# Decay masks of a chunked state-space scan: one-sum broadcasts by DMA and a ScalarE bias in place of selector matmuls

## The chip, the cores and the metric

The kernel runs on one core of a Trainium2 chip. The metric is the device time of one execution in microseconds. The engines named below are PE (TensorE matmuls), PEld (TensorE weight loads), DVE (VectorE), ACT (ScalarE), POOL (GpSimd) and SP (SyncE, which only issues DMAs here).

## The reference: what is computed

One decoder layer over 1024 positions and 1024 channels: a layer norm, a wide input projection, two parallel mixers (a gated 31-tap convolution and a Mamba-2 scan), a gated sum with an output projection and a layer norm, and then a convolutional feed-forward block. The change touches the scan alone:

```
a = dt * a_head                               # (chunk, position, head), all negative
a_cs = cumsum(a over the 128 positions of a chunk)
seg[l, s] = a_cs[l] - a_cs[s]
decay = where(l >= s, exp(seg), 0)            # per head
y_diag = (C B^T * decay) @ (x * dt)           # per group of 8 heads
y_off  = exp(a_cs) * (C @ state)
state  = exp(a_cs[last]) * state + (B * exp(a_cs[last] - a_cs))^T (x * dt)
```

There are 32 heads in 4 groups of 8, a head has 64 channels, a state has 128 rows, and a chunk has 128 positions, so 8 chunks.

## The kernel before, in words

The sequence is worked in two halves of 512 positions (4 chunks each), index `hh`. For each half, `mixers` (L653) makes the projections of the input. A projection of 128 channels is 24 matmuls of 128x512: 8 blocks of the inner dimension, each as three products of a high and a low part in the format float32r (`mm3`, L193 to 198; `project`, L200). Weights are loaded by SP, copied to the high part by ACT (L172) and subtracted to the low part by DVE (L173), into tiles that rotate over three buffers.

After the first columns, `time_steps` (L308) makes the time steps and, with `upper`, the running sums `a_cs` of every head (L361). It forms `a` with every head repeated four times, so that the 128 rows of the sum are (group, kind 0 to 3, head). The sum is split into a high part (L373) and a low part (L375), and two tables come out of it: `seg_mv` (negated high and low parts, and ones) and `seg_st` (ones, and high and low parts), by L378 and L381.

For each of the four groups the mixer then makes its columns, the gates of the other mixer's convolution (`glu`), and `ssd_group` (L507), which loops over the half's four chunks. Per chunk and group (32 of them in all) it does this:

- PE transposes x and B (L531, L534) and multiplies B with C (L537) into PSUM.
- POOL makes, for group 0, the moving operand `au` (128x1024): `seg_mv` kept in the rows of each head and zeroed elsewhere (L540); it is stored to DRAM (L546) and loaded again for groups 1 to 3 (L548). ACT makes the stationary operand `sg` (L550), the rows of `seg_st` of this group.
- Two matmuls of 128x512 (L554) select and add: their result is `a_cs[s] - a_cs[l]` for 8 heads. ACT applies Relu out of PSUM (L562) and Exp with scale -1 (L563) to the tile `m`, 128x1024. Relu keeps the exponent at zero above the diagonal, where the mask is zero anyway.
- DVE masks B C^T by `upper` (L565), scales x (L567, L572) and multiplies `m` with the masked product (L575). PE multiplies with the state (L580), makes the new state (L584) and multiplies `m` with x (L594, 8 heads).

At the head of each group, `ys` is loaded with exp(a_cs), broadcast over partitions from the DRAM tile `e_scr` (L513); `normed` later passes a row through DRAM and back (L632, L633). These and the loads of `au` are all issued by POOL, in one order. The convolution of 31 taps (`conv31`, L483, 480 instructions on DVE) runs with a lower priority between all this, and `combine` reads its result.

The order of the instructions on every engine is made by a planner, which simulates the program with a cost model and gives each engine a fixed order by priorities and by when an operand would be ready; weight loads have a high priority. Only the PE order of the feed-forward's first part is written by hand. An engine works its list in order, and a waiting instruction holds back what stands behind it.

Of the kernel before, what the change touches and what calls it, by code (L numbers as in the profile page):

```python
# [8 lines left out]
F32 = mybir.dt.float32  # L9
# [45 lines left out]
def kernel(  # L55
# [30 lines left out]
    def bank(which):  # L86
# [18 lines left out]
    V.memset(ones, 1.0)  # L105
    eps = const.tile([P, 1], F32, name="eps")
    V.memset(eps, EPS)
    head_of = const.tile([P, GROUPS, 8], F32, name="head_of")
    V.tensor_reduce(
        out=head_of,  # L110
        in_=ident.rearrange("p (g k h) -> p g h k", k=4, h=8),
        axis=AX.X,
        op=ALU.add,
    )
    lanes = statep.tile([P, 16], F32, name="lanes")
    head_all, group_of = lanes[:, :8], lanes[:, 8:12]
    V.tensor_reduce(
        out=head_all, in_=head_of.rearrange("p g h -> p h g"), axis=AX.X, op=ALU.add
    )
    V.tensor_reduce(out=group_of, in_=head_of, axis=AX.X, op=ALU.add)  # L120
    kind = const.tile([P, 4], F32, name="kind")
    V.tensor_reduce(
        out=kind, in_=ident.rearrange("p (g k h) -> p k g h", k=4, h=8), axis=AX.XY, op=ALU.add
    )
    kind_mv = const.tile([P, 1], F32, name="kind_mv")
    V.tensor_add(kind_mv, kind[:, 2:3], kind[:, 3:4])
    kind_st = const.tile([P, 1], F32, name="kind_st")
    V.tensor_add(kind_st, kind[:, 0:1], kind[:, 1:2])
    kind_neg = const.tile([P, 2], F32, name="kind_neg")
    V.tensor_scalar_mul(kind_neg, kind[:, 0:2], -1.0)  # L130
    pc = const.tile([P, PC_N + 24], F32, name="pc")
    a_log = statep.tile([P, HEADS], F32, name="a_log")
    nskip = statep.tile([P, 2, 16], F32, name="nskip")
    pick = statep.tile([P, 4, 4], F32, name="pick")
# [1 line left out]
    for c in range(4):  # L136
# [7 lines left out]
    states = [statep.tile([P, HALF], F32, name=f"state{g}") for g in range(GROUPS)]  # L144
    dts = [statep.tile([P, 4, HEADS], F32, name=n) for n in ("dtv", "wds")]
    edc = statep.tile([P, 2, 4, HEADS], F32, name="edc")
    seg_mv = statep.tile([P, 4, P], F32, name="seg_mv")
    seg_st = statep.tile([P, 4, P], F32R, name="seg_st")

    h_scr = [dram.tile([HALF, D], F32, name=f"h_scr{i}") for i in range(2)]  # L150
    h1_scr = dram.tile([T, D], F32, name="h1_scr")
# [5 lines left out]
    )  # L157
    c_scr = [dram.tile([8, P, HALF], F32, name=f"c_scr{i}") for i in range(2)]
    g_scr = [dram.tile([8, P, HALF], F32, name=f"g_scr{i}") for i in range(2)]
    e_scr = [dram.tile([P, HALF], F32, name=f"e_scr{i}") for i in range(2)]  # L160
    au_scr = [
        [dram.tile([P, 8 * P], F32R, name=f"au_scr{i}_{c}") for c in range(4)] for i in range(2)
    ]
    r_scr = [dram.tile([GROUPS, HALF], F32, name=f"r_scr{i}") for i in range(2)]
    y_scr = [dram.tile([8, P, HALF], F32, name=f"y_scr{i}") for i in range(2)]

# [141 lines left out]
    def time_steps(pl, hh, ps):  # L308

        n2 = 2 * HEADS  # L310
        dtc = pl.tile([n2, HALF], F32, tag="yo", bufs=2, name=f"dtc{hh}")
        A.activation(
            out=dtc, in_=ps[:n2, :], func=AF.Identity, bias=pc[:n2, PC_DTB : PC_DTB + 1]
        )
        pt = bank(0)
        for c in range(4):
            TE.matmul(
                pt[:, c * HEADS : (c + 1) * HEADS],
                dtc[:, c * P : (c + 1) * P],
                fold,  # L320
                start=True,
                stop=True,
            )
        n = 4 * HEADS
        dtv, wds = (d.rearrange("p c h -> p (c h)") for d in dts)
        work = pl.tile([P, 8 * P], F32, tag="m", name=f"sp{hh}")
        v, s, s2, q, a = (work[:, i * n : (i + 1) * n] for i in range(5))
        ea = work[:, 5 * n : 6 * n + HEADS]
        e = ea[:, :n]
        V.tensor_scalar_mul(ea[:, n:], a_log, -1.0)  # L330
        V.tensor_copy(v, pt[:, :n])
        A.activation(out=e, in_=v, func=AF.Abs)
        A.activation(out=ea, in_=ea, func=AF.Exp, scale=-1.0)
        V.tensor_scalar_add(s, e, 2.0)
        V.reciprocal(out=s, in_=s)
        V.tensor_mul(s, s, e)
        V.tensor_mul(s2, s, s)
        V.tensor_scalar(
            out=q, in0=s2, scalar1=1.0 / 17.0, scalar2=1.0 / 15.0, op0=ALU.mult, op1=ALU.add
        )  # L340
        for k in (13, 11, 9, 7, 5, 3):
            V.tensor_mul(q, q, s2)
            V.tensor_scalar_add(q, q, 1.0 / k)
        V.tensor_mul(q, q, s2)
        V.scalar_tensor_tensor(out=q, in0=q, scalar=1.0, in1=s, op0=ALU.add, op1=ALU.mult)
        V.tensor_scalar_max(v, v, 0.0)
        V.scalar_tensor_tensor(out=dtv, in0=q, scalar=2.0, in1=v, op0=ALU.mult, op1=ALU.add)
        V.scalar_tensor_tensor(
            out=a.rearrange("p (c h) -> p c h", c=4),
            in0=dts[0],  # L350
            scalar=-1.0,
            in1=ea[:, n:].unsqueeze(1).to_broadcast([P, 4, HEADS]),
            op0=ALU.mult,
            op1=ALU.mult,
        )
        ax = pl.tile([P, 4, GROUPS, 4, 8], F32, tag="xs", name=f"sp_ax{hh}")
        for k in range(4):
            A.copy(ax[:, :, :, k, :], a.rearrange("p (c g h) -> p c g h", c=4, g=GROUPS))
        pa = bank(0)
        for c in range(4):  # L360
            TE.matmul(  # L361
                pa[:, c * P : (c + 1) * P],
                ax[:, c].rearrange("p g k h -> p (g k h)"),
                upper,
                start=True,
                stop=True,
            )
        eh = pl.tile([P, HALF], F32, tag="yo", bufs=2, name=f"sp_eh{hh}")
        A.activation(out=eh, in_=pa, func=AF.Exp)
        G.dma_start(e_scr[hh], eh)  # L370
        hi = pl.tile([P, HALF], F32R, tag="xsd", name=f"sp_hi{hh}")
        lo = pl.tile([P, HALF], F32, tag="sig", name=f"sp_lo{hh}")
        V.tensor_copy(hi, pa)  # L373
        hi = hi.bitcast(F32)
        V.tensor_tensor(out=lo, in0=pa, in1=hi, op=ALU.subtract)  # L375
        for dst, m, const_m in ((seg_mv, kind_neg, kind_mv), (seg_st, kind[:, 2:4], kind_st)):
            part = pl.tile([P, HALF], F32, tag="ya", bufs=2, name=f"sp_part{hh}")
            V.tensor_scalar(  # L378
                out=part, in0=hi, scalar1=m[:, 0:1], scalar2=const_m, op0=ALU.mult, op1=ALU.add
            )  # L380
            V.scalar_tensor_tensor(  # L381
                out=dst.rearrange("p c l -> p (c l)"),
                in0=lo,
                scalar=m[:, 1:2],
                in1=part,
                op0=ALU.mult,
                op1=ALU.add,
            )
        pe = bank(0)
        for i, m in enumerate((later, ones)):  # L390
            TE.matmul(pe[:, i * n : (i + 1) * n], m, a, start=True, stop=True)
        ev = edc.rearrange("p i c h -> p (i c h)")
        A.activation(out=ev, in_=pe[:, : 2 * n], func=AF.Exp)
        V.tensor_mul(wds, dtv, edc[:, 0].rearrange("p c h -> p (c h)"))
# [112 lines left out]
    def ssd_group(pl, hh, g, xT, BT, CT, gate):  # L507
        S = states[g]
        h8 = slice(8 * g, 8 * g + 8)
        acc = pl.tile([P, 4, HALF], F32, tag="ys", name=f"ys{hh}_{g}")  # L510
        ev = e_scr[hh].rearrange("(g k i j) t -> g k j i t", k=4, j=2, i=4)
        for j in range(2):
            G.dma_start(acc[j * HP : (j + 1) * HP], ev[g, 0, j].partition_broadcast(HP))  # L513

        def heads(t):
            return t.rearrange("p (h q) -> p h q", h=8)
# [7 lines left out]
        for c in range(4):  # L524
# [10 lines left out]
                bt = pl.tile([P, P], F32, tag="bt", name=f"bt{nm}")  # L535
                A.copy(bt, pb[:, :P])
            TE.matmul(pb[:, P : 2 * P], BT[:, cs], CT[:, cs], start=True, stop=True)  # L537
            au = pl.tile([P, 8, P], F32R, tag="au", name=f"au{nm}")
            if g == 0:
                G.tensor_tensor(  # L540
                    out=au,
                    in0=seg_mv[:, c, :].unsqueeze(1).to_broadcast([P, 8, P]),
                    in1=head_all.unsqueeze(2).to_broadcast([P, 8, P]),
                    op=ALU.mult,
                )
                G.dma_start(au_scr[hh][c], au.rearrange("p h l -> p (h l)"))  # L546
            else:
                G.dma_start(au.rearrange("p h l -> p (h l)"), au_scr[hh][c])  # L548
            sg = pl.tile([P, P], F32R, tag="sg", name=f"sg{nm}")
            A.mul(sg, seg_st[:, c, :].bitcast(F32), group_of[:, g : g + 1])  # L550
            m = pl.tile([P, 8, P], F32, tag="m", name=f"m{nm}")
            for q in range(2):
                pg = bank(0)
                TE.matmul(  # L554
                    pg,
                    sg,
                    au[:, 4 * q : 4 * q + 4, :].rearrange("p h l -> p (h l)"),
                    start=True,
                    stop=True,
                )  # L560
                mq = m[:, 4 * q : 4 * q + 4, :].rearrange("p h l -> p (h l)")
                A.activation(out=mq, in_=pg, func=AF.Relu)  # L562
                A.activation(out=mq, in_=mq, func=AF.Exp, scale=-1.0)  # L563
            cbm = pl.tile([P, P], F32, tag="cbm", name=f"cbm{nm}")
            V.tensor_mul(cbm, pb[:, P : 2 * P], upper)  # L565
            xs = pl.tile([P, HALF], F32, tag="xs", name=f"xs{nm}")
# [798 lines left out]
```

## Time and profile before

| | |
|---|---|
| median of 3 runs | 1968.07 us (1966.53 to 1968.48) |
| the profiled execution, its own time | 1967.68 us |
| its span | 1966.0 us |
| PE busy | 1938.1 us, 99% |
| PEld busy | 1591.8 us, 81% |
| DVE busy | 1666.4 us, 85% |
| ACT busy | 1069.9 us, 54% |
| POOL busy | 153.0 us, 8% |

The span is the profile's stretch from the first to the last instruction; the time of the execution has 1.7 us around it. A matmul's shown duration reaches into the next one's, because matmuls are pipelined: what a matmul takes of PE's time is the distance from its start to the next start. A row of a group gives the line, engine, operation, output and inputs with shapes and the count, then the busy time and the mean of one, then the idle time ahead of it and what ended it.

### The profile page before, as it was taken

What the parts mean: (1) busy time and instruction counts of PE and PEld (TensorE: products, weight loads), DVE (VectorE), ACT (ScalarE), POOL (GpSimd) and SP (SyncE); (2) the same over time, 40 slices, a digit from 0 to 9 for tenths busy, and PEclk for the clock granted to TensorE, in tenths of its full rate; (3) what the DMA queues carried; (4) which work ended last, traced back from release to release, by engine and by line L of the source; (5) the groups of instructions that cost most, each with busy time, mean ns of one, the idle gap of its engine ahead of it and who ended that gap; (6) DMA issues with size and microseconds to landing.
All of it is one profiled execution on the core that took longest, in us unless ns stands there. A gap on an engine that the chain in (4) does not pass through costs nothing.

```text
span 1966.0 us, 24887 instructions
## 1 busy us (share of the span) xinstructions
PE 1938.1 (99%) x9240; PEld 1591.8 (81%) x9240; DVE 1666.4 (85%) x2256; ACT 1069.9 (54%) x1521; POOL 153.0 (8%) x185
## 2 busy tenths in 40 slices
PE   7999999999999999999999999999999999999997
PEld 6888888888888888888888888888778888888886
DVE  7899999999666879999999967588998887878868
ACT  5676666466453365776745546365655454553442
POOL 1110000000400011000000032001000000011000
PEclk9999999999999999999999999999999999999999
DMA  6434343534545542434353354477452232368572
GB/s 221 134 107 125 108 131 116 161 118 140 171 134 185 224 132 97 142 119 125 108 166 122 120 182 129 146 277 257 140 171 98 101 123 86 107 229 266 187 250 107
DMA packets 103848, 297.92 MB, mean 152 GB/s; under 512 B 12240, under 2 KB 12272, under 8 KB 103728
## 3 DMA queue, kind: packets, MB, share of 16 engines
q1 hardware_dynamic: 87840, 244.68, 36.7%
q0 software_dynamic: 13584, 47.47, 7.9%
q10 hardware_dynamic: 2304, 4.20, 0.6%
q8 instruction: 72, 1.18, 0.2%
q14 instruction: 48, 0.39, 0.1%
HBM read 242.02 MB, written 54.28 MB: 151 GB/s over the span
## 4 chain that ended last, share of the span: by engine, by line
PE 95%; DVE 3%; issue 1%; DMA 1%; ACT 0%; SPq 0%; DVEq 0%; ACTq 0%
PE acc L198 25%; PE acc L196 25%; PE acc L197 25%; PE sm L197 4%; PE sm L196 4%; PE sm L198 4%; PE sm L594 2%; PE sm L580 1%; PE sm L584 1%; PE acc L420 1%; PE sm L531 1%; PE sm L554 1%; DVE rows L270 1%; DVE rows L273 0%; PE acc L410 0%
## 5 line engine op out<-in xcount | busy, mean ns | idle before, releaser
L483 DVE SCALAR_TENSOR_TENSOR c<-v,pc,c 128x512 f32<-128x512 f32 x480 | 347.6, 752 | 3.6 <-ACT c L472 2.9
L197 PE MATMUL acc<-hT,w_c 128*128 128x512 f32 x352 | 139.5, 396 | 0.0
L196 PE MATMUL acc<-hT,w_c 128*128 128x512 f32 x352 | 139.2, 395 | 0.0
L198 PE MATMUL acc<-hT,w_c 128*128 128x512 f32 x352 | 138.7, 394 | 0.0
L1004 DVE SCALAR_TENSOR_TENSOR fo<-u,pc,fo 128x1024 f32<-128x1024 f32 x88 | 111.4, 1285 | 0.4 <-ACT fo L1000 0.4
L438 DVE SCALAR_TENSOR_TENSOR xbc<-u,pc,xbc 128x512 f32<-128x512 f32 x144 | 106.4, 754 | 0.5 <-ACT xbc L436 0.4
L196 PE MATMUL acc<-h1s,w_s 128*128 128x512 f32 x264 | 103.3, 391 | 2.3 <-ACT u L988 2.3
L198 PE MATMUL acc<-h1s,w_s 128*128 128x512 f32 x264 | 103.0, 390 | 0.0
L197 PE MATMUL acc<-h1s,w_s 128*128 128x512 f32 x264 | 102.7, 389 | 0.0
L198 PE MATMUL acc<-hT,w_z 128*128 128x512 f32 x256 | 102.2, 399 | 0.0
L196 PE MATMUL acc<-hT,w_z 128*128 128x512 f32 x256 | 101.0, 394 | 0.0
L197 PE MATMUL acc<-hT,w_z 128*128 128x512 f32 x256 | 100.8, 394 | 0.0
L1143 ACT CAST w_dn<-dr 128x1024 fp32r<-128x1024 f32 (+1 forms) x73 | 60.9, 843 | 71.5 <-DVE dr L1073 36.9
L172 ACT CAST w_c<-st_c 128x1024 fp32r<-128x1024 f32 x48 | 50.4, 1049 | 71.1 <-PE acc L198 52.0
L1144 DVE TENSOR_TENSOR w_dn<-dr,w_dn 128x1024 fp32r<-128x1024 f32 (+1 forms) x73 | 70.0, 968 | 13.3 <-ACT w_dn L1143 13.1
L198 PEld LDWEIGHTS acc<-hT,w_c 128*128 128x128 f32 x352 | 66.1, 188 | 15.3 <-issue 1.9
L197 PEld LDWEIGHTS acc<-hT,w_c 128*128 128x128 f32 x352 | 66.2, 188 | 15.0 <-issue 1.9
L196 PEld LDWEIGHTS acc<-hT,w_c 128*128 128x128 f32 x352 | 66.2, 188 | 14.5 <-issue 1.4
L196 PE MATMUL sm<-h1b,w_s 128*128 128x512 f32 x176 | 69.1, 393 | 0.0
L197 PE MATMUL sm<-h1b,w_s 128*128 128x512 f32 x176 | 69.0, 392 | 0.0
L198 PE MATMUL sm<-h1b,w_s 128*128 128x512 f32 x176 | 69.0, 392 | 0.0
L196 PE MATMUL acc<-h1b,w_ue 128*128 128x512 f32 x168 | 65.6, 390 | 0.9 <-ACT first L926 0.9
(377 smaller groups left out, 5668.6 us busy)
## 6 DMA issues: line engine op xcount, KB each, us to landing
st_c<-wcol SPq DMA_DIRECT2D x50, 512.0 KB, 3.6
st_z<-wz SPq DMA_DIRECT2D x32, 512.0 KB, 3.5
au<-au_scr POOLq DMA_DIRECT2D x24, 512.0 KB, 4.0
st_wo<-wo SPq DMA_DIRECT2D x24, 512.0 KB, 4.0
ra<-wup SPq DMA_DIRECT2D x22, 512.0 KB, 3.5
rb<-wup SPq DMA_DIRECT2D x22, 512.0 KB, 3.4
t_scr<-fo POOLq DMA_DIRECT2D x22, 512.0 KB, 3.4
dr<-t_scr SPq DMA_DIRECT2D x44, 256.0 KB, 3.8
```

The costliest lines, as they stand in the source:

```text
L172: A.copy(w[:, 0, :], st)
L196: TE.matmul(ps, wa(0), xa(0), start=start, stop=False, skip_group_check=more)
L197: TE.matmul(ps, wa(0), xa(1), start=False, stop=False, skip_group_check=more)
L198: TE.matmul(ps, wa(1), xa(0), start=False, stop=stop, skip_group_check=more)
L270: V.scalar_tensor_tensor(out=t, in0=t, scalar=mv[:, i, 0:1], in1=g, op0=op, op1=ALU.mult)
L420: TE.matmul(ps[:, ts], w[:, i, k * P : (k + 1) * P], hT[:, j, k, ts], start=n == 0 and k == 0, stop=n == 2 and k == KD - 1,)
L438: V.scalar_tensor_tensor(out=o, in0=u[:, k : k + HALF], scalar=pc[:, wc + k : wc + k + 1], in1=o, op0=ALU.mult, op1=ALU.add,)
L483: V.scalar_tensor_tensor(out=accs[i], in0=v[:, k : k + HALF], scalar=pc[:, wc + k : wc + k + 1], in1=accs[i], op0=ALU.mult, op1=ALU.add,)
L594: TE.matmul(py[h % 2 * HP : (h % 2 + 1) * HP, h // 2 * P : (h // 2 + 1) * P], xs[:, h * HP : (h + 1) * HP], m[:, h, :], start=True, stop=True,
L1004: V.scalar_tensor_tensor(out=o, in0=u[:, k : k + T], scalar=pc[:, wc + k : wc + k + 1], in1=o, op0=ALU.mult, op1=ALU.add,)
L1143: A.copy(w[:, 0, cs], src)
L1144: V.tensor_tensor(out=w[:, 1, cs], in0=src, in1=w[:, 0, cs].bitcast(F32), op=ALU.subtract)
```

## The change

`time_steps` no longer repeats the heads. The running sums are 32 rows (head) by 512 (chunk, position) in PSUM. DVE copies them to SBUF (`cum`), POOL stores them by four small DMAs to a DRAM tile ordered by group, chunk, head and position, and four small matmuls with the identity turn them round, so that `cums` holds for each position (partition) its own sum of each chunk and head. Per chunk and group one DMA broadcasts the 8 heads' sums (1024 numbers, 4 KB) to all 128 partitions, straight into `m`, which now has two buffers. ACT then applies, for each of the 8 heads, Relu with scale -1 and the partition's own sum as bias, in place, and one Exp over all of `m`. The tables `seg_mv` and `seg_st`, the selectors, `au`, `sg`, and the two matmuls of L554 are gone. `pc` is made wider by the room that the small constants had.

```diff
-    head_of, lanes, kind, kind_mv, kind_st, kind_neg ...
-    pc = const.tile([P, PC_N + 24], F32, name="pc")
+    pc = const.tile([P, PC_N + 88], F32, name="pc")
-    seg_mv = statep.tile([P, 4, P], F32, name="seg_mv")
-    seg_st = statep.tile([P, 4, P], F32R, name="seg_st")
+    cums = statep.tile([P, 4, HEADS], F32, name="cums")
-    e_scr = [dram.tile([P, HALF], F32, name=f"e_scr{i}") for i in range(2)]
-    au_scr = ...
+    e_scr = [dram.tile([HEADS, HALF], F32, name=f"e_scr{i}") for i in range(2)]
+    cum_scr = [dram.tile([GROUPS, 4, 8, P], F32, name=f"cum_scr{i}") for i in range(2)]
 # time_steps
-        ax = pl.tile([P, 4, GROUPS, 4, 8], F32, tag="xs", name=f"sp_ax{hh}")
-        for k in range(4):
-            A.copy(ax[:, :, :, k, :], a.rearrange("p (c g h) -> p c g h", c=4, g=GROUPS))
         pa = bank(0)
         for c in range(4):
             TE.matmul(
-                pa[:, c * P : (c + 1) * P],
-                ax[:, c].rearrange("p g k h -> p (g k h)"),
+                pa[:HEADS, c * P : (c + 1) * P],
+                a[:, c * HEADS : (c + 1) * HEADS],
                 upper, start=True, stop=True,
             )
+        eh = pl.tile([HEADS, HALF], F32, tag="yo", bufs=2, name=f"sp_eh{hh}")
+        cum = pl.tile([HEADS, HALF], F32, tag="xsd", name=f"sp_cum{hh}")
+        A.activation(out=eh, in_=pa[:HEADS], func=AF.Exp)
+        V.tensor_copy(cum, pa[:HEADS])
+        for g in range(GROUPS):
+            G.dma_start(
+                cum_scr[hh][g].rearrange("c h l -> h c l"),
+                cum[8 * g : 8 * g + 8].rearrange("h (c l) -> h c l", c=4),
+            )
         G.dma_start(e_scr[hh], eh)
-        hi, lo, part, seg_mv, seg_st: six instructions on DVE
+        pc_t = bank(0)
+        for c in range(4):
+            TE.matmul(
+                pc_t[:, c * HEADS : (c + 1) * HEADS],
+                cum[:, c * P : (c + 1) * P],
+                ident[:HEADS, :HEADS], start=True, stop=True,
+            )
+        V.tensor_copy(cums.rearrange("p c h -> p (c h)"), pc_t[:, :n])
 # ssd_group, per chunk
-            au, sg, and for q in range(2): TE.matmul(pg, sg, au...), Relu, Exp
+            m = pl.tile([P, 8, P], F32, tag="m", bufs=2, name=f"m{nm}")
+            mf = m.rearrange("p h l -> p (h l)")
+            G.dma_start(
+                mf, cum_scr[hh][g, c].rearrange("h l -> (h l)").partition_broadcast(P)
+            )
+            for h in range(8):
+                k = 8 * g + h
+                A.activation(
+                    out=m[:, h, :], in_=m[:, h, :], func=AF.Relu, scale=-1.0,
+                    bias=cums[:, c, k : k + 1],
+                )
+            A.activation(out=mf, in_=mf, func=AF.Exp, scale=-1.0)
```

More of the change, by code (lines that the diff above doesn't have):

```diff
@@ L107 @@
     V.memset(eps, EPS)
[L108 to L130, printed above, removed]
-    pc = const.tile([P, PC_N + 24], F32, name="pc")
+    pc = const.tile([P, PC_N + 88], F32, name="pc")
     a_log = statep.tile([P, HEADS], F32, name="a_log")
@@ L159 @@
     g_scr = [dram.tile([8, P, HALF], F32, name=f"g_scr{i}") for i in range(2)]
-    e_scr = [dram.tile([P, HALF], F32, name=f"e_scr{i}") for i in range(2)]
-    au_scr = [
-        [dram.tile([P, 8 * P], F32R, name=f"au_scr{i}_{c}") for c in range(4)] for i in range(2)
-    ]
+    e_scr = [dram.tile([HEADS, HALF], F32, name=f"e_scr{i}") for i in range(2)]
+    cum_scr = [dram.tile([GROUPS, 4, 8, P], F32, name=f"cum_scr{i}") for i in range(2)]
     r_scr = [dram.tile([GROUPS, HALF], F32, name=f"r_scr{i}") for i in range(2)]
@@ L325, in time_steps @@
         dtv, wds = (d.rearrange("p c h -> p (c h)") for d in dts)
-        work = pl.tile([P, 8 * P], F32, tag="m", name=f"sp{hh}")
+        work = pl.tile([P, 8 * P], F32, tag="m", bufs=2, name=f"sp{hh}")
         v, s, s2, q, a = (work[:, i * n : (i + 1) * n] for i in range(5))
@@ L367, in time_steps @@
             )
-        eh = pl.tile([P, HALF], F32, tag="yo", bufs=2, name=f"sp_eh{hh}")
-        A.activation(out=eh, in_=pa, func=AF.Exp)
-        G.dma_start(e_scr[hh], eh)
[L371 to L379, printed above, removed]
-            )
[L381 to L388, printed above, removed]
+        eh = pl.tile([HEADS, HALF], F32, tag="yo", bufs=2, name=f"sp_eh{hh}")
[7 more added lines that the diff above has]
+            )
+        G.dma_start(e_scr[hh], eh)
+        pc_t = bank(0)
[3 more added lines that the diff above has]
+                cum[:, c * P : (c + 1) * P],
+                ident[:HEADS, :HEADS],
+                start=True,
+                stop=True,
+            )
+        V.tensor_copy(cums.rearrange("p c h -> p (c h)"), pc_t[:, :n])
         pe = bank(0)
@@ L510, in ssd_group @@
         acc = pl.tile([P, 4, HALF], F32, tag="ys", name=f"ys{hh}_{g}")
-        ev = e_scr[hh].rearrange("(g k i j) t -> g k j i t", k=4, j=2, i=4)
+        ev = e_scr[hh].rearrange("(g i j) t -> g j i t", j=2, i=4)
         for j in range(2):
-            G.dma_start(acc[j * HP : (j + 1) * HP], ev[g, 0, j].partition_broadcast(HP))
+            G.dma_start(acc[j * HP : (j + 1) * HP], ev[g, j].partition_broadcast(HP))
         def heads(t):
@@ L537, in ssd_group @@
             TE.matmul(pb[:, P : 2 * P], BT[:, cs], CT[:, cs], start=True, stop=True)
[L538 to L544, printed above, removed]
-                )
[L546 to L563, printed above, removed]
+            m = pl.tile([P, 8, P], F32, tag="m", bufs=2, name=f"m{nm}")
[8 more added lines that the diff above has]
+                    bias=cums[:, c, k : k + 1],
+                )
+            A.activation(out=mf, in_=mf, func=AF.Exp, scale=-1.0)
             cbm = pl.tile([P, P], F32, tag="cbm", name=f"cbm{nm}")
```

## The prediction, made before the changed kernel had run

> **What bounds the kernel now.** I read the page's busy shares and chain first, then the waits of PE, then busy time by stage.
>
> ```profile
> span 1966.0 us, 24887 instructions
> PE 1938.1 (99%) x9240; PEld 1591.8 (81%) x9240; DVE 1666.4 (85%) x2256; ACT 1069.9 (54%) x1521; POOL 153.0 (8%) x185
> ...
> PE 95%; DVE 3%; issue 1%; DMA 1%; ACT 0%; SPq 0%; DVEq 0%; ACTq 0%
> ```
>
> PE is busy for 99% of the span and carries 95% of the chain that ended last. Its longest wait (total, times, longest) is at the start of the program:
>
> ```profile
> PE sm L222 <- DVE x L273: 13.7, 2, 12.4
> ```
>
> The scan lies in the two mixers; their stretches, with busy time of PE, PEld, DVE, ACT and POOL, and then PE's granted clock:
>
> ```profile
> 60.00:490.00 430.00, 430.00 (x2156) 348.41 (x2155) 405.15 (x566) 273.55 (x412) 26.21 (x35) 1.00 0.40 127
> 720.00:1140.00 420.00, 420.00 (x2135) 342.32 (x2135) 402.77 (x561) 264.86 (x372) 25.60 (x35) 1.00 0.41 128
> ```
>
> PE never pauses there, at full clock. DVE is at 94 and 96%, ACT at 64 and 63%. So what shortens the list of PE shortens the run, as long as no other engine then makes PE wait.
>
> **What PE loses.** The two selector matmuls per chunk, 64 in all. The busy time of their group counts overlapping durations, so I take starts from the timeline around the first pair and around a single one:
>
> ```profile
> L554 PE MATMUL sm<-au,sg 128*128 128x512 f32 x64 | 28.1, 448 | 0.0
> ```
> ```profile
> 83.12 0.71 PE L554 MATMUL sm<-au,sg 128*128 128x512 f32 x2
> 83.67 0.39 PE L196 MATMUL acc<-hT,w_z 128*128 128x512 f32 x1
> 83.90 0.40 PE L197 MATMUL acc<-hT,w_z 128*128 128x512 f32 x1
> ...
> 98.69 0.48 PE L554 MATMUL sm<-au,sg 128*128 128x512 f32 x1
> 99.00 0.40 PE L196 MATMUL acc<-hT,w_z 128*128 128x512 f32 x1
> ```
>
> The pair takes 83.67 - 83.12 = 0.55 us, 0.275 each; the single one 0.31. A projection's matmul takes 0.23 (83.90 - 83.67). The bounds for 64 are 64 x 0.23 = 14.7 and 64 x 0.31 = 19.8 us; I take 0.285 between the two forms, **18.2 us**.
>
> The group row's 28.1 us would be the answer for whoever reads busy time as cost. The Trainium skill (Perfetto Trace Analysis, Identifying the Most-Contended Engine) warns against exactly that row: matmul busy time does not tell how close TensorE is to its limit, and the share of LDWEIGHTS should be used. By the page's measure, 81%, a fifth of TensorE would be free and the removal could be worth nothing; I carry that as a rival below, while the even 0.23 us steps speak against it.
>
> **What PE gets.** Four matmuls per half that turn the sums round (contraction over 32 heads, 32 columns out). The nearest row is L317 of the same function, also four float32 matmuls with 32 columns, each recorded as two:
>
> ```profile
> 36.77 0.40 PE L197 MATMUL acc<-hT,w_c 128*128 128x512 f32 x1
> 37.10 1.07 PE L317 MATMUL sm<-fold,dtc 64*128 64x32 f32 x8
> 38.10 0.50 PE L198 MATMUL acc<-hT,w_c 128*128 128x512 f32 x1
> ```
>
> From 37.10 to 38.10 it is 1.0 us, and the matmul ahead takes 0.33 in place of 0.23: 1.1 us per half, **2.2 us** together. The running sums themselves (L361, below) keep their count and their 128 moving columns and get a narrower stationary operand: 63.17 to 64.06 is 0.89 us per half now; the gain is between 0 and 0.9 each, and I take 0. PE's list thus shrinks by 18.2 - 2.2 = **16.0 us**, bounds 14.7 - 2.2 = 12.5 and 19.8 - 2.2 + 1.8 = 19.4.
>
> **What ACT loses and gets.** The writers of the mask `m` (minimum, median and maximum of one; first and last start), and three groups:
>
> ```profile
> L562 ACT ACTIVATE m<-sm x64: 572/598/612, 84.5 to 1111.8; 128x512 f32<-128x512 f32 x64
> L563 ACT ACTIVATE m<-m x64: 616/632/637, 87.2 to 1112.5; 128x512 f32<-128x512 f32 x64
> L575 DVE TENSOR_TENSOR m<-m,cbm x32: 1205/1218/1226, 91.7 to 1114.0; 128x1024 f32<-128x1024 f32 x32
> ```
> ```profile
> L563 ACT ACT_TABLE_LOAD x45 | 57.7, 1283 | 0.8
> ...
> L172 ACT CAST w_c<-st_c 128x1024 fp32r<-128x1024 f32 x48 | 50.4, 1049 | 71.1 <-PE acc L198 52.0 <-issue 9.5 <-DVE mv_o L251 4.4
> ...
> L550 ACT ACTIVATE sg<-seg_st,lanes 128x128 fp32r<-128x128 f32 x32 | 12.8, 401 | 0.5 <-DVE seg_st L381 0.5
> ```
>
> Gone per chunk: 2 x 0.598 + 2 x 0.632 + 0.401 = 2.86 us. New: eight Relu of 128x128 with a per-partition operand, and one Exp of 128x1024. L550 is the nearest row for a Relu, since it has the size and such an operand: 0.401; a quarter of L562, 0.15, is the other bound. For the Exp I take the cast of that size, 1.05. Together 8 x 0.401 + 1.05 = 4.26 us (at least 2.25), so 1.40 us more per chunk and 32 x 1.40 = 45 us in all. The table loads fall from 45 to at most 32, since there is one Exp per chunk: 13 x 1.283 = 17 us less. ACT in the mixers goes from 538 to about 566 of 850 us, 67%. It hides as long as the weight casts (L172) aren't late, which stand on ACT with the burst. While a third weight tile is being filled, two are ahead: 48 matmuls at 0.23, 11 us. The cast (1.05) and the subtraction on DVE (L173, of the size of L575, 1.22) leave 8.7 us. The longest burst is 4.26 + 1.28 = 5.5 us, so it fits; and ACT waits 52.0 us for PE at L172, so the casts are early today. Cost: 0.
>
> **What moves onto DMA.** The exponents now come by a broadcast load of 512 KB per chunk, issued by POOL, in place of the load of `au` of that size.
>
> ```profile
> au<-au_scr POOLq DMA_DIRECT2D x24, 512.0 KB, 4.0
> ...
> e_scr<-sp_eh POOLq DMA_DIRECT2D x2, 256.0 KB, 2.8
> ln_g<-prow POOLq DMA_DIRECT2D x1, 512.0 KB, 7.0
> ```
>
> The new load writes 512 KB from 4 KB of source, as `ln_g` does: between 4.0 and 7.0 us to land, I take 7. In number, 32 such loads and 8 stores of 16 KB replace 24 loads and 8 stores of 512 KB, so the DMA engines (0.40 and 0.41 busy in the mixers' rows) see no more. The first two chunks lie 98.69 - 83.12 = 15.6 us apart. With two buffers a load may start when the chunk two before has ended its products (L594). Issue 0.6, landing 7, burst 5.5, product on DVE 1.22 and its place in that list: 15 us against 31. It stands on POOL behind `ys` and the stores of `normed`, as `au` did; those are waits that the second buffer now covers by a chunk. Cost: 0. If the buffer came round late, each chunk would lose what exceeds 31 us.
>
> **The start of a half** has no such lead:
>
> ```profile
> 63.17 1.05 PE L361 MATMUL sm<-upper,sp_ax 128*128 128x128 f32 x8
> ...
> 64.06 0.39 PE L391 MATMUL sm<-sp,later 128*128 128x128 f32 x2
> ```
> ```profile
> L373 DVE CAST sp_hi<-sm x2: 691/692/692, 64.9 to 722.5; 128x512 fp32r<-128x512 f32 x2
> ```
> ```profile
> L548 POOL DMA_DIRECT2D au<-au_scr x24 | 13.1, 544 | 369.3 <-PE sm L554 313.1 <-PE sm L537 53.5 <-PE acc L198 2.3
> ```
> ```profile
> 97.14 1.09 PE L594 MATMUL sm<-m,xs 128*64 128x128 f32 x16
> ...
> 745.85 1.09 PE L594 MATMUL sm<-m,xs 128*64 128x128 f32 x16
> ```
>
> The copy of the sums takes the place of L373, at 64.9 and 722.5. An issue takes POOL 0.54 (L548), say 0.6. From there: 0.7 copy, five stores (3.0), 2.8 until the last has landed, two issues of `ys` (1.2), 0.6 and 7.0 for the load, 4.3 + 1.3 on ACT, 1.2 on DVE: 22.1 us. The first product starts 32.2 us after it in the first half and 23.3 us in the second. It fits, in the second by 1 us; if it comes 2 or 3 us late PE waits that once. Cost: 0, at most 3.
>
> **DVE and POOL.** Per half DVE drops six passes over 128x512 (L373, L375, and L378 and L381 twice; at L373's 0.69 about 4.1 us) and gets one like L373 and one over a quarter of that, about 0.9: some 3 us less. POOL drops the eight products of L540. DVE is what is late next: PE gives back 8 us per half, and DVE has 25 and 17 us free in the mixers. Were its convolutions to end no sooner than now, their normed result `sT` would still be in time:
>
> ```profile
> 566.50 1.29 DVE L213 TENSOR_TENSOR sT<-cc,sT 128x512 fp32r<-128x512 f32 x2
> ...
> 578.08 0.39 PE L196 MATMUL acc<-sT,w_co 128*128 128x512 f32 x1
> ```
>
> It is made by 567.8, and PE asks for it at 578.1, or at 570 after the change.
>
> **Sum.** Against the profiled execution's own time: 1967.68 - 18.2 + 2.2 = 1951.7. The median of the runs shown is 0.4 above that execution, so **1952 us**, 0.8% faster.
>
> **Rivals.**
> (a) *The new order loses part of it.* The planner makes every engine's list anew, and L594 already waits 11.3 us for the weights that it multiplies:
>
> ```profile
> L594 PEld LDWEIGHTS sm<-m,xs 128*64 128x64 f32 x512 | 27.3, 136 | 11.3 <-issue 5.6 <-DVE c L483 2.8 <-DVE xbc L438 0.7
> ```
>
> If each of 32 chunks lost 0.25 us more there, 8 us, the time is 1960. For it: DVE at 95%, with the convolution's steps (L483) ahead of it in the waits. Against: `m` no longer waits for PE, so it is ready sooner.
> (b) *PE is not the bound*, by the share of weight loads: 81%, and the matmuls taken out were filling gaps. The time is then 1966 to 1969, no change. Against it, PE shows 430 of 430 us busy and no waits.
> (c) *ACT holds the weights back: slower.* The burst of nine stands on ACT in order and waits for a DMA; what it delays are the casts of L172, then L173, then PE. It decides once burst and wait exceed 8.7 us, so if the load lands over 3 us late. Priced at half of the 45 us of extra ACT work reaching PE: 1952 + 22 = 1974. Against it: a chunk's load has 31 us.
> (d) *The change does more.* If part of L594's waits goes too (they are 11.3 us, say half), with the upper bound of the removal: 1968 - 19.4 - 5.5 = 1943.
> That the change doesn't do what it says (the matmuls stay) has no ground in the diff.
>
> **How the numbers follow.** The forecast (1948 to 1956) has 0.56, (a) 0.16, (b) 0.06, (c) 0.12, (d) 0.10. A measurement of this kernel tells about 0.2%, 4 us, from no change. Faster: forecast, (d) and nearly all of (a): 0.81. Same: (b) and a bit of (a): 0.07. Slower: 0.12. The range leaves out (c) and the far half of (d) and of (b): 1944 to 1967.
>
> **What would show it.** Right: no L554, PE still without waits in both mixers, the mixers' stretch shorter by 8 us each, L594's weight loads waiting about 11 us in total, about 32 table loads at Exp, ACT at 67% there. Wrong: PE waiting at L594 for DVE's product or at L196 for L173 (rival c), POOL's loads landing later than 15 us after the buffer came free, PE waiting for `sT`, or the mixers unchanged in length with PE idle in them (b).

## The result and the profile after

| | before | after |
|---|---|---|
| median of 10 runs each | 1968.09 us (1966.35 to 1969.34) | 1962.74 us (1960.62 to 1964.00) |
| the profiled execution, its own time | 1967.68 us | 1963.25 us |
| its span | 1966.0 us | 1961.5 us |

The ratio is 0.9974, with a 95% interval of 0.9965 to 0.9983: the change makes the kernel faster by about 5 us. The forecast was 16 us. The direction was right and the time lies in the range given, but two thirds of the gain are missing. Ratios from here on are to runs of the kernel before on the same chip at the same time; every time is a median, but for the one single run that is named.

The page of the changed kernel, its busy shares and chain:

```profile
PE 1929.1 (98%) x9192; PEld 1581.7 (81%) x9192; DVE 1649.3 (84%) x2241; ACT 1061.8 (54%) x1617; POOL 137.5 (7%) x185
...
PE 88%; DVE 6%; DMA 3%; ACT 2%; issue 1%; SPq 0%; DVEq 0%; ACTq 0%; POOLq 0%
```

PE's share of the chain fell from 95% to 88%, so now other engines stand on the path. The waits of PE (total, times, longest) say where; of these rows only the first had a counterpart before, of 2.3 us in total, 1.2 the longest:

```profile
PE acc L170 <- ACT u L944: 3.3, 2, 2.1
PE acc L171 <- DVE yT L187: 2.1, 2, 1.4
PE acc L170 <- ACT w_wo L146: 0.9, 1, 0.9
```

The scan itself is not among them. Busy time by stretch, as in the prediction (PE, PEld, DVE, ACT, POOL, then PE's granted clock), shows PE still without a pause in the first mixer and within half a microsecond of it in the second:

```profile
60.00:490.00 430.00, 430.00 (x2159) 348.09 (x2158) 400.79 (x563) 272.19 (x465) 20.09 (x35) 1.00 0.41 129
720.00:1140.00 420.00, 419.50 (x2134) 340.84 (x2133) 395.13 (x557) 260.03 (x425) 21.05 (x37) 1.00 0.40 130
```

The starts of all PE matmuls give an account of the span from the first start to the last. The distance from each start to the next is summed by what the matmul is. Where a projection's matmul takes over 0.15 us more than its usual distance, the excess is counted as a wait; matmuls 0.42 us apart instead of 0.23 are the half-speed ones told of below. What is left when waits and half speed are taken off is called PE's list.

| part of PE's time, change from before to after | forecast | measured |
|---|---|---|
| selector matmuls | -18.2 | -18.3 |
| turning matmuls | +2.2 | +2.0 |
| transposes of B, which stood ahead of a selector | 0 | +1.9 |
| projections between a short matmul and a projection | 0 | +3.2 |
| all else in the list | 0 | -0.2 |
| **PE's list** | **-16.0** | **-11.4** |
| waits (3.7 to 9.2 us) | 0 | +5.5 |
| half-speed matmuls (0.2 to 1.8 us) | 0 | +1.6 |
| **sum** | **-16.0** | **-4.3** |

The spans differ by 4.5 us. So the missing gain has two parts: 4.6 us that the list never lost, and 7.1 us of new waits and slow matmuls behind it. The experiments take these in turn.

### The profile page after: what moved, and what is told of

Read it like the earlier page. It is cut to its first block, busy times and chain, and to the rows that moved or that the text cites. A ratio compares the mean times of both kernels' runs of the same rounds, so it can differ in the third digit from the quotient of the medians.

```text
span 1961.5 us, 24877 instructions
## 1 busy us (share of the span) xinstructions
PE 1929.1 (98%) x9192; PEld 1581.7 (81%) x9192; DVE 1649.3 (84%) x2241; ACT 1061.8 (54%) x1617; POOL 137.5 (7%) x185
## 4 chain that ended last, share of the span: by engine, by line
PE 88%; DVE 6%; DMA 3%; ACT 2%; issue 1%; SPq 0%; DVEq 0%; ACTq 0%; POOLq 0%
PE acc L172 23%; PE acc L170 23%; PE acc L171 23%; PE sm L170 3%; PE sm L172 3%; PE sm L171 3%; PE sm L550 1%; PE acc L390 1%; PE sm L536 1%; PE sm L540 1%; DVE c L453 1%; PE sm L501 1%; DVE xbc L408 1%; DVE rows L244 1%; DMA st_wo<-wo 0%
## 5 line engine op out<-in xcount | busy, mean ns | idle before, releaser
L453 DVE SCALAR_TENSOR_TENSOR c<-v,pc,c 128x512 f32<-128x512 f32 x480 | 343.4, 745 | 1.9 <-ACT c L442 1.0
L515 ACT ACTIVATE m<-m,cums 128x128 f32<-128x128 f32 x256 | 78.8, 390 | 75.1 <-DMA m<-cum_scr 67.4
```

The lines of the kernel that those rows point to most:

```text
L453: V.scalar_tensor_tensor(out=accs[i], in0=v[:, k : k + HALF], scalar=pc[:, wc + k : wc + k + 1], in1=accs[i], op0=ALU.mult, op1=ALU.add,)
L515: A.activation(out=m[:, h, :], in_=m[:, h, :], func=AF.Relu, scale=-1.0, bias=cums[:, c, k : k + 1],)
```

## Experiments

### What is a selector worth: two such matmuls put back

An edit of the changed kernel, per chunk, with results that nothing reads:

```diff
             TE.matmul(pb[:, P : 2 * P], BT[:, cs], CT[:, cs], start=True, stop=True)
+            for q in range(2):
+                TE.matmul(bank(0), hT[:, 0, q, :P], hT[:, 0, q, :], start=True, stop=True)
```

> The changed kernel with two unread matmuls of 128x512 per chunk put where the selectors stood (after B times C); nothing else is given back, and their result isn't used. Theory L (the list): a selector pair also took over the 0.08 us in which the next projection's weights can't be hidden, so a selector is worth 0.227 us, and 64 of them make PE's list longer by 14 to 15 us (sum of the distances from one start to the next, waits over 0.3 us left out). Theory P (the prediction's): each is worth 0.285, 18.2 us. In time, L gives 1962.7 + 14.5 = 1977, P 1981, each give or take 4 us for the waits of a list made anew; the sum over the trace decides.

Measured: 1971.06 us, a ratio to before of 1.0018 (1.0009 to 1.0026), 8.3 us above the changed kernel. The list, by the same account, is 14.4 us longer than the changed kernel's: 14.4 / 64 = 0.225 us for each matmul, the 0.23 that was the lower bound. The time rose by less, and stayed below both forecasts, because the planner made the list anew and the waits and slow matmuls in it fell, from 11.0 to 6.0 us. The added pair, in the group row and in the timeline of this kernel:

```profile
L509 PE MATMUL sm<-hT 128*128 128x512 f32 x64 | 26.7, 428 | 0.0
```
```profile
85.23 0.71 PE L509 MATMUL sm<-hT 128*128 128x512 f32 x2
85.78 0.39 PE L170 MATMUL acc<-hT,w_z 128*128 128x512 f32 x1
```

The pair takes 85.78 - 85.23 = 0.55 us here too, as the selectors did, and yet costs 0.45. The timeline of the changed kernel, at a place where a selector used to stand, shows why:

```profile
103.28 0.27 PE L504 MATMUL sm<-ident,xbc 128*128 128x128 f32 x1
103.39 1.06 PE L536 MATMUL sm<-xbc,state 128*128 128x128 f32 x8
104.20 0.47 PE L171 MATMUL acc<-hT,w_z 128*128 128x512 f32 x1
104.52 0.39 PE L172 MATMUL acc<-hT,w_z 128*128 128x512 f32 x1
104.75 0.39 PE L170 MATMUL acc<-hT,w_z 128*128 128x512 f32 x1
```

A projection matmul that follows matmuls of 128 columns takes 104.52 - 104.20 = 0.32 us, the next one 0.23. The weight loads (PEld) of the same place show where the difference lies:

```profile
104.29 0.19 PEld L172 LDWEIGHTS acc<-hT,w_z 128*128 128x128 f32 x1
104.52 0.19 PEld L170 LDWEIGHTS acc<-hT,w_z 128*128 128x128 f32 x1
```

Each matmul starts 0.23 us after its own weight load. Further on that load starts together with the matmul ahead (104.52); here it starts 0.09 us behind it (104.29 for 104.20). So the first wide matmul behind short ones pays 0.09 us, whichever it is. A selector in that place paid it; without the selector the projection behind pays it. Such projections went from 9 to 28 behind the matmuls with the state (L536) and from 7 to 25 behind B times C (L507): 37 x 0.086 = 3.2 us. The last transpose pays likewise: in the kernel before, the selector started 0.03 us after it,

```profile
98.66 0.27 PE L534 MATMUL sm<-ident,xbc 128*128 128x128 f32 x1
```

(98.69 in the prediction's rows), and now the next matmul starts 103.39 - 103.28 = 0.11 us after it.

### Is ScalarE on the path: every Relu twice

```diff
                     bias=cums[:, c, k : k + 1],
                 )
+                A.activation(out=m[:, h, :], in_=m[:, h, :], func=AF.Relu)
```

> The changed kernel with a second Relu without bias behind each of the 256, which changes no value: some 256 x 0.3 = 77 us more work for ScalarE in the mixers, and a burst per chunk that is 2.4 us longer. Theory L and W: ScalarE stays hidden, since the mask is done 10 to 60 us ahead of its use; 1959 to 1967. Rival C (the burst holds back the weight casts and so PE): slower than the changed kernel by at least 5 us, with PE waiting for weight casts or for their subtraction.

Measured: 1962.26 us, a ratio of 0.9972 (0.9961 to 0.9982), the same as the changed kernel. ACT's busy time rose from 1061.8 to 1108.7 us, by 47 us and not the 77 expected, and cost nothing. Rival (c) falls.

### Does one more projection cover the wait: a gate moved

The wait for `yT` (L187) is in `combine`, at 502 us, where the second half of `wssm` meets the last group's normed result. The edit gives PE the third gate projection ahead of the first product, in the changed kernel and, with the same lines, in the kernel before:

```diff
-            gate(0)
-            gate(1)
+            for j in range(3):
+                gate(j)
             for j in range(8):
-                if 0 < j < 7:
-                    gate(j + 1)
+                if 0 < j < 6:
+                    gate(j + 2)
```

> The changed kernel with the third projection of the second gate moved ahead of the first product of the combine stage; same work. It changes what lies between the sum of squares of the last group and the products that need its normed result, where PE waited 2.3 us in the first half. Theory W (waits of re-made lists): PE's list keeps its length within 0.5 us, and the waits over 0.3 us change by some us in either direction; 1958 to 1966. Theory D (VectorE is the bound of the mixers' end): the wait at that place stays or moves to the next operand of VectorE, 2 to 3 us again.

> The kernel before with the same move of the third gate projection; same work. Theory W: its time moves by as much as that of the changed kernel does, within 4 us of 1968, since its waits too belong to the list. Theory D: no change, since the kernel before has no wait for VectorE there.

Measured: 1962.00 us (ratio 0.9974, 0.9963 to 0.9984) and 1969.55 us (1.0005, 0.9996 to 1.0014): no change in either. The wait in the changed kernel stayed, at 2.6 us, as theory D had it, but not for the reason that it gives. The order of PE's matmuls in the two traces explains it: in the changed kernel `gb_2` had already stood between the mean squares of the last group (`pick`, L580) and the first matmul that needs its `yT`. The move only exchanged it with the products of the other half of `yT`, so 40 projection matmuls lie between the two with the edit and without. In the kernel before there are 60. That made the next pair of runs.

### What sets the wait for yT: the place of four matmuls in PE's list

In the changed kernel `pick` stands behind the 20th of 24 matmuls of `gb_1`. This is PE there:

```profile
491.94 1.04 PE L580 MATMUL sm<-ss,pick 128*4 128x128 f32 x8
...
502.12 0.47 PE L170 MATMUL acc<-yT,w_sp 128*128 128x512 f32 x1
504.03 0.50 PE L171 MATMUL acc<-yT,w_sp 128*128 128x512 f32 x1 [1.43 <-DVE yT L187]
...
506.37 0.50 PE L171 MATMUL acc<-yT,w_sp 128*128 128x512 f32 x1 [0.67 <-DVE yT L187]
```

and DVE, which made the last sum of squares, then waited for the row that comes back through DRAM, and made `yT`:

```profile
485.57 0.69 DVE L575 TENSOR_TENSOR ss<-ss,sq 128x512 f32<-128x512 f32 x1
500.64 2.74 DVE L592 SCALAR_TENSOR_TENSOR xbc<-xbc,nskip,ss 128x512 f32<-128x512 f32 x4 [4.19 <-DMA ss<-r_scr]
503.29 1.28 DVE L187 TENSOR_TENSOR yT<-xbc,yT 128x512 fp32r<-128x512 f32 x2
```

The sum is whole at 486.3 us, but PE takes it up at 491.94. From there to the start of the first `yT` on DVE is 11.4 us, and PE has 10.2 us of other work. In the kernel before, `pick` stands ahead of all of `gb_1`, and PE asks 14.7 us after it, at 508.27:

```profile
493.55 1.04 PE L624 MATMUL sm<-ss,pick 128*4 128x128 f32 x8
```
```profile
508.27 0.39 PE L196 MATMUL acc<-yT,w_sp 128*128 128x512 f32 x1
```

Two runs move nothing else of note on PE (beside the four matmuls of `pick` only two pairs for means and variances change places, later on). In the changed kernel a scheduling dependency with no wait makes the first matmul of `gb_1` follow `pick`; in the kernel before, another makes `pick` follow the 19th matmul of `gb_1`, in the first half alone. The lines that hand `picked`, `late` and `m0` on are left out.

```diff
 # changed kernel
-                project(pg, weights(wcol[CT_GB + j], f"gb{hh}_{j}"), hT)
+                project(pg, weights(wcol[CT_GB + j], f"gb{hh}_{j}"), hT, picked[0] if j == 1 else None)
 # in project, after the first product of block k
+            if after is not None and k == 0:
+                tc.add_manual_dep(
+                    m0.ins, after.ins.name,
+                    mb_.DependencyInfo(mb_.DependencyClass.NoSync, mb_.DependencyReason.DATA),
+                    reason="order",
+                )
 # kernel before: late = first matmul of pick
+            if late is not None and k == 6:
+                tc.add_manual_dep(late.ins, m0.ins.name, ...)
```

> The changed kernel with one order pinned on TensorE: the four matmuls that take the mean squares of the last group (tile pick) stand ahead of the projection gb_1 in both halves. In the first half of the changed kernel they stand behind 20 of the 24 matmuls of gb_1, at 492 us, though ss is whole at 486.3 us; 40 projection matmuls (4, 12 and 24, some 9.1 us at 0.227) are left between them and the first matmul that reads the last group's yT, and 60 (13.6 us) with the pin. In the second half they already stand ahead of gb_1, so nothing moves there. Theory N: the new wait at 502 us comes of this place in the list, since the chain from the four matmuls to yT takes about 11.2 us: the wait (2.5 us in the changed kernel's trace, 2.8 us and half speed behind it in two of the variants) goes to under 0.3 us, and the time to 1958.5 to 1960.5 us. Theory V, that VectorE's backlog sets when yT comes: the four multiplications that make yT come no earlier than now, a wait of 2 us or more stays, 1961.5 to 1963.5 us.

> The kernel before with the same four matmuls pinned late in the first half alone: behind the 19th matmul of gb_1 instead of ahead of gb_1, so that 41 projection matmuls (9.3 us) are left between them and the first use of the last group's yT, and not 60. Theory N: the wait that the changed kernel has at 502 us is made in the kernel before too, 2 to 3 us at about 508 us, time 1970 to 1972.5 us. Theory V (VectorE's backlog, less in the changed kernel than here): the four matmuls' place is not what decides, wait under 0.5 us and 1968 us, since yT was ready 0.9 us early and comes by VectorE's own pace.

Measured: the changed kernel with `pick` early takes **1958.47 us**, a ratio of 0.9947 (0.9934 to 0.9960), whose interval lies below the changed kernel's. The wait is gone; PE and DVE there (lines are one to nine higher than in the changed kernel):

```profile
486.34 1.04 PE L589 MATMUL sm<-ss,pick 128*4 128x128 f32 x8
...
501.06 0.39 PE L171 MATMUL acc<-yT,w_sp 128*128 128x512 f32 x1
```
```profile
499.00 2.49 DVE L196 TENSOR_TENSOR yT<-xbc,yT 128x512 fp32r<-128x512 f32 x4
```

The kernel before with `pick` late takes 1970.99 us (ratio 1.0014, 1.0004 to 1.0023), 2.7 us more than before, and has the wait that it never had:

```profile
497.81 1.04 PE L633 MATMUL sm<-ss,pick 128*4 128x128 f32 x8
```
```profile
509.60 0.50 PE L197 MATMUL acc<-yT,w_sp 128*128 128x512 f32 x1 [1.22 <-ACT yT L221]
511.54 0.50 PE L198 MATMUL acc<-yT,w_sp 128*128 128x512 f32 x1 [1.44 <-DVE yT L222]
```

Theory N holds both ways, and V falls: DVE did its part in time as soon as PE did. The gain of 4.3 us is more than the 2.5 us of the wait. In the starts of the two profiled executions, which lie 5.4 us apart at the end, 2.8 us of it fall to this place, 1.7 us to the place at 1410 us, where this execution has no half-speed matmuls, and 1.1 us to the very start, where it was granted the full clock at 17.0 us instead of 20.8; the start has nothing to do with `pick`. The wait at 1410 us is still there, at 1.9 us.

All 14 traces sort by this one count. The six with 40 to 43 projection matmuls between `pick` and the first use (the changed kernel, a gate moved, every Relu twice, `pick` late, and 36 or 12 small matmuls, told of below) wait 2.4 to 4.0 us there; the eight with 53 or 60 do not wait.

### What sets the wait at 1410 us: a fetch of instructions amid a load

In the feed-forward's first part SP loads `s` from `first_scr` (L929), ACT copies it into PSUM (L931), and PE waits for ACT. Rows of the changed kernel's SP and ACT, and the landing time of that load, in us:

```profile
1404.61 0.32 SPq L929 DMA_DIRECT2D s<-first_scr  x1
```
```profile
1411.44 0.59 ACT L931 COPY acc<-s 128x512 f32<-128x512 f32 x1 [4.23 <-DMA s<-first_scr]
```
```profile
DMA to landing us min/median/max: 6.8/6.8/6.8
```

The same load in the kernel before, issued at the same point of the work:

```profile
1411.35 0.32 SPq L973 DMA_DIRECT2D s<-first_scr  x1
```
```profile
1415.94 0.59 ACT L975 COPY acc<-s 128x512 f32<-128x512 f32 x1 [1.99 <-DMA s<-first_scr]
```
```profile
DMA to landing us min/median/max: 4.6/4.6/4.6
```

The bytes moved in the 10 us around it are the same but for one row, which only the changed kernel has there (from the DMA queues between 1402 and 1412 us: packets, MB, share of 16 engines):

```profile
q8 instruction: 1, 0.02, 0.6%
```

It is one packet of 16 KB. The page counts them for the whole run:

```profile
q8 instruction: 72, 1.18, 0.3%
```

72 is what PE's 18,484 instructions in the records (matmuls, weight loads and the few beside them) give at 256 each, so I read them as fetches of PE's own instructions. The same quotient, rounded down, is the count of packets in all 14 traces (73 in the kernel before with 35, 37 or 70 more matmuls), and moving them by PE's count, below, bears it out. The changed kernel has 103 fewer of those instructions than before, so a fetch falls at another point of the work: here 3.1 us behind the issue of the load. Small unread matmuls at the very start, where PE otherwise waits until 12.7 us, move the fetches:

```diff
+    with tc.high_priority(offset=9000):
+        for q in range(36):
+            pd = bank(0) if q % 16 == 0 else pd
+            o = q % 16 * HEADS
+            TE.matmul(pd[:, o : o + HEADS], ident[: 2 * HEADS], fold, start=True, stop=True)
     hT = ln_in(0)
```

> The changed kernel with 36 more small matmuls (fold on the identity, 128x32, read by nothing) at the very start, where TensorE otherwise idles until 12.7 us. They shift each fetch of TensorE's instructions (16 KB for 256 instructions, about 28 us apart) about 72 instructions, some 8 us, ahead of the work. In the changed kernel one such fetch lands amid the load of s from first_scr that was issued at 1404.6 us, and the load takes 6.8 us instead of 4.6 us. Theory F, that the fetch delays the load: the wait of TensorE at about 1410 us goes from 2.0 to 2.4 us (three runs of the changed kernel's family) to 1.3 us, as in the kernel before, and no half-speed matmuls stand behind it; the time 0.7 to 2.5 us below the changed kernel's if the start is no slower, 1960 to 1963 us in all. Theory G, that the transfers collide among themselves: the wait stays at 2.0 us or more.

> The changed kernel with 12 of the small matmuls at the start instead of 36: as the run with 36 showed, each is two passes of 0.216 us, so they are 48 instructions and end at about 7 us, ahead of the first transpose at 12.7 us, and the lists of all engines are otherwise those of the changed kernel. The fetch of TensorE's instructions that fell 3 us behind the issue of the load of s comes about 5.4 us earlier in the work, 2 us ahead of that issue. Theory F (the fetch delays the load): the wait at about 1410 us is 1.3 us as with 36, no half speed behind it, and the wait at 502 us stays; time 1960 to 1962 us, 0.7 to 2.5 us less than the changed kernel. Theory G: the wait is 2.0 us or more again, since what mended it in the run with 36 was the other order at the start; time 1962.7 us.

Measured: with 36 of them 1964.96 us (ratio 0.9982, 0.9973 to 0.9991), since they filled more than the idle time and put the start off by 4.7 us, but the wait at this place is 1.33 us and the fetch 16 us off. With 12 of them, and all other orders as they were, 1959.78 us (0.9962, 0.9949 to 0.9974), the wait 1.33 us, and the load back at its old time:

```profile
DMA to landing us min/median/max: 4.5/4.5/4.5
```

Theory F holds for the wait. For the time the run with 12 decides nothing: its interval overlaps the changed kernel's, its wait for `yT` came out longer (3.3 us and half speed behind it), and its work begins 1.7 us earlier, with the full clock granted at 15.2 us instead of 20.8.

The other way round, into the kernel before:

> The kernel before with 70 of the small matmuls at the start, which move the fetches of TensorE's instructions 140 instructions ahead, so that one falls about 3 us behind the issue of the load of s from first_scr at 1411.4 us, where the changed kernel has it. Theory F: that load takes 6 us or more instead of 4.6 us, and TensorE's wait at about 1417 us goes from 1.3 to 2.0 to 2.4 us, perhaps with half-speed matmuls behind it; time 1968.5 to 1973 us, up to 3 us of it from the start, which the trace tells apart. Theory G: the wait stays at 1.3 us.

> The kernel before with 35 of the small matmuls at the start (70 passes, 140 instructions): the run with 70 of them moved the fetches by 280 instructions, more than the 256 that lie between two of them, so that none fell on the load and nothing was tried there. With 140 a fetch falls some 3 us behind the issue of the load of s, in the work where the kernel before has it at 1411.4 us. Theory F: that load takes 6 us or more instead of 4.6 us, and the wait of TensorE behind it 1.9 to 2.4 us instead of 1.33 us. Theory G: 1.33 us. The start is some 5 us later by the small matmuls, so the time (1973 to 1977 us) tells nothing.

> The kernel before with 37 of the small matmuls at the start. With 35 the fetch of TensorE's instructions fell 4.0 us behind the issue of the load of s (4.6 us to landing, wait 1.33 us); in the changed kernel's family it fell 2.5 to 3.2 us behind it (6.4 to 7.0 us to landing, wait 1.9 to 2.4 us). Two more, 8 instructions, bring it to about 3.1 us. Theory F: the load lands 6 us or more after its issue, and the wait of TensorE behind it is 1.9 to 2.4 us. Theory G: 4.6 us and 1.33 us. The start is some 5 us later, so the time (1973 to 1978 us) tells nothing.

The first two missed their aim. With 70 the fetches moved by more than a whole period (1986.84 us, nearly all of it from the start; the wait 1.33 us), and with 35 the fetch fell 4.0 us behind the issue (1974.55 us; landing 4.6 us, wait 1.33 us): too late to touch the load. With 37 it fell 2.2 us behind (1976.47 us, a single run), and the load was late in the kernel before, too. The runs with 35 and 37 differ by two small matmuls and the places of a few instructions, so the other order at the start that both have is not the cause. The landing and ACT's row with 37:

```profile
DMA to landing us min/median/max: 6.0/6.0/6.0
```
```profile
1425.94 0.59 ACT L975 COPY acc<-s 128x512 f32<-128x512 f32 x1 [3.42 <-DMA s<-first_scr]
```

But PE's wait was 1.47 us and not 1.9: the forecast of that run holds for the load and not for the wait. A load 1.4 us late cost PE 0.14 us, and one 2.2 us late (4.6 to 6.8) cost 0.95 us; so PE has about 1.3 us to spare there. The three variants of the changed kernel that kept the late load agree: 1.9, 1.9 and 2.4 us late, they cost 0.59, 0.65 and 1.11 us.

### Both together

> The kernel with the four matmuls of the last group pinned ahead of gb_1, and the 12 small matmuls at the start. If both causes hold and add, the waits of TensorE at 502 us and over 1.4 us at 1410 us are both gone, and the time is 1958.5 us (the pin alone) less 0.6 us (a wait of 1.92 us that goes to 1.33 us): 1957 to 1958.5 us. If the pin's gain of 4.3 us already holds all that the half-speed stretch cost, no less than 1958 us.

Measured: **1957.12 us**, a ratio of 0.9939 (0.9925 to 0.9952), the fastest of all, though not told apart from `pick` early alone. No half-speed matmuls are left and the waits are 5.3 us. What the list gave, 11.4 us off the profiled 1967.68, would be 1956.3.

## Why the prediction was wrong, step by step

Two steps failed: the worth of a selector, which leaves 4.6 us in PE's list, and the waits of PE, which the prediction put at nothing and which came to 7.1 us with the half speed behind them. That ACT, DMA and the start of a half cost nothing held.

- **What PE loses: mis-sized.** The 0.285 us for a selector was its true distance to the next start (18.3 us measured for 64), but not its worth. That distance held 0.06 us of a cost that belongs to the place behind short matmuls and passed on to the next one. The lower bound, 0.23 from a projection's matmul, was right: 0.225 by putting them back. The choice "between the two forms" cost 3.8 us of the forecast, and the list's sum 4.6.
- **What PE gets: right.** Two groups of four turning matmuls took 2.0 us for a forecast of 2.2:

```profile
L351 PE MATMUL sm<-ident,sp_cum x16: 271/271/292, 69.4 to 725.1; 32*128 32x32 f32 x16
```

- **ACT: the cost of 0 was right, the size was not.** ACT did not rise to 67% of the mixers but fell from 538 to 532 of 850 us, 63%. The eight Relu have a mean of 0.390 us, as L550 had, but overlap: 78.8 us busy for 256 is 0.31 each. And the table loads went to 29 instead of 32:

```profile
L515 ACT ACTIVATE m<-m,cums 128x128 f32<-128x128 f32 x256 | 78.8, 390 | 75.1 <-DMA m<-cum_scr 67.4 <-DVE state L544 6.9 <-DVE w_z L147 0.7
L519 ACT ACT_TABLE_LOAD x29 | 37.2, 1283 | 0.5
```

- **DMA and the start of a half: right at 0.** The broadcast landed in 4.7 us, near the lower bound. ACT's first Exp of the run starts at 85.3 us and DVE multiplies that mask at 97.5:

```profile
m<-cum_scr POOLq DMA_DIRECT2D x32, 512.0 KB, 4.7
```
```profile
L519 ACT ACTIVATE m<-m x32: 1042/1062/1066, 85.3 to 1091.3; 128x1024 f32<-128x1024 f32 x32
L531 DVE TENSOR_TENSOR m<-m,cbm x32: 1206/1219/1226, 97.5 to 1099.8; 128x1024 f32<-128x1024 f32 x32
```

- **"DVE is what is late next": the step that failed.** It checked one consumer, `sT`, at 567.8 against 570, and took the rest as covered. The late one was `yT` of the last group. In the kernel before DVE begins it at 506.11, and PE asks at 508.27, with 0.6 us for the first of its four blocks, so it was less than 2 us from being late:

```profile
506.11 2.49 DVE L213 TENSOR_TENSOR yT<-xbc,yT 128x512 fp32r<-128x512 f32 x4
```

And it hung less on DVE than on where PE's own list put `pick`. The sum assumed that the new lists keep such places; the planner moved this one 20 matmuls back, 2.5 us of wait. For the place at 1410 us the prediction has no term at all: 0.95 us more of wait and 1.6 us of half speed. DVE's load fell somewhat more than the 3 us per half that were forecast: 405.15 to 400.79 us and 402.77 to 395.13 us in the mixers.
- **Rival (a) had the kind of cause, not the place.** The new order did lose several us, but not at the weights of the masks, which wait 11.3 us as before (L550, was L594):

```profile
L550 PEld LDWEIGHTS sm<-m,xs 128*64 128x64 f32 x512 | 27.3, 136 | 11.3 <-issue 10.2 <-PE acc L172 0.4 <-DVE yT L187 0.4
```

- **Rival (b) falls.** 64 matmuls put back made the list 14.4 us longer and the time 8.3. PEld's share, 81%, is what it was, while PE's list set the time. The rule of the Trainium skill (Perfetto Trace Analysis, Identifying the Most-Contended Engine), that the headroom of TensorE is judged by MFU (the share of its peak arithmetic that is used) and by that share, does not agree with these runs as far as the share goes.
- **Rival (d) falls:** no wait went away, and the removal came out at its lower bound.

What stays open: the waits for the weights of the output projection (`w_wo`, 1275 to 1300 us). They are 1.4 us in the changed kernel's trace and 0 in the one before, but between 0 and 2.3 us in the variants of either; no run was aimed at them, nor at 0.7 us for the gate `sig` at 906 us. So 2.1 of the 7.1 us have no cause that is shown.

## What to carry to other kernels

Value a matmul that is taken out by the steady distance between its neighbours, and ask which matmul will pay for a late weight load in its place; its own distance to the next start is too much. Where lists are made anew, count for each engine that returns work to the bound one, not only how much it has to do, but how many instructions of the bound engine lie between the hand-over and the first use: 60 became 40 here, and that place was worth 2.8 us in the trace of the changed kernel and 4.2 us in that of the kernel before. A pinned order can win it back without touching the work.

## What the runs showed of the hardware

**The granted clock halved for one window of 3.41 us behind a window in which PE idled 1.9 us or more.** Behind the wait at 1410 us the changed kernel's matmuls start 0.42 us apart instead of 0.23:

```profile
1410.58 0.39 PE L172 MATMUL acc<-h1s,w_s 128*128 128x512 f32 x1
1413.08 0.53 PE L170 MATMUL acc<-h1s,w_s 128*128 128x512 f32 x1 [2.12 <-ACT u L944]
...
1414.26 0.63 PE L170 MATMUL acc<-h1s,w_s 128*128 128x512 f32 x1
1414.69 0.63 PE L171 MATMUL acc<-h1s,w_s 128*128 128x512 f32 x1
```

Stretches cut at the changes of the clock record (PE's busy time is the second number; the granted clock the one behind POOL):

```profile
1410.02:1413.43 3.41, 1.29 (x7) 0.74 (x6) 2.65 (x4) 1.99 (x4) 0.00 (x0) 1.00 0.24 48
1413.43:1416.84 3.41, 3.41 (x10) 2.65 (x9) 2.91 (x4) 0.65 (x1) 0.55 (x1) 0.50 0.14 55
1416.84:1420.25 3.41, 3.41 (x17) 2.82 (x16) 1.23 (x1) 2.50 (x3) 0.00 (x0) 1.00 0.18 70
```

In all 14 traces, from the first grant of the full clock to the last matmul, such a drop happened four times, each one window long, and began a whole number of windows (142, 143, 143, 408) after the full clock was first granted. The windows ahead of the four drops held 1.93 to 2.58 us of PE idle; the largest idle time in a window without a drop behind it was 1.76 us amid the work, and 1.87 us where the last matmul ends (every Relu twice). So a wait of 2 us costs 1.6 us more if it falls into one window, and not if it straddles two: the kernel before with `pick` late idled 2.7 us in two neighbouring windows, 1.1 and 1.6, and kept its clock. The Trainium skill (TensorE: Matmul & The Clock Gate, The HAM clock gate) states a free-running window of 3413 ns, and the traces agree. The same page of the Trainium skill (Why this matters for your kernels) advises against idle gaps of over about 3 us between bursts of matmuls, and here 1.93 us within one window were enough.

**A fetch of PE's instructions delays a load that it meets.** In the five traces where it fell 2.2 to 3.2 us behind the issue of that one load of 256 KB (the changed kernel, three of its variants, and the kernel before with 37 small matmuls), the load took 6.0 to 7.0 us; in the other nine, 4.5 to 4.6 us. The loads issued within 1.8 us of it were late with it (`ra`, 6.8 us in the changed kernel and 5.1 before). The packet itself took 0.96 us in the changed kernel's trace, so how it comes to cost 2 us is not shown. So a change of the number of instructions alone can move a wait, with no change to the work around it.
